# Ten two-input operations of a hybrid SSD and latent-attention layer made on GpSimd instead of VectorE

## The chip, the core and the metric

The kernel runs on one core of a Trainium2 chip. The metric is the device time in microseconds of one execution; three runs of the kernel before gave a median of 635.32 us (635.25 to 635.61). The core's engines run side by side, each through its own queue in order: TensorE (PE: matrix products, with weight loads shown apart as PEld), VectorE (DVE), ScalarE (ACT), GpSimd (POOL) and SyncE (SP, which only issues DMAs here). An instruction that needs another engine's result waits for a semaphore, and all that stands behind it on its queue waits too.

## The reference, cut to what matters

One layer of an encoder for 512 new frames and 64 frames of a running stream (576 tokens together, model width 1024): state-space heads (SSD) and latent attention side by side, then a dense SwiGLU block. The parts that the change touches:

```python
def step(h, inp):                       # one chunk of the state-space scan
    ...
    y = y + jnp.einsum('blgn,bghpn,blgh->blghp', Ck, h, jnp.exp(cum))
    last = cum[:, -1]
    w_end = jnp.exp(last[:, None] - cum) * d
    h_new = jnp.exp(last)[..., None, None] * h + jnp.einsum('blgh,blghp,blgn->bghpn', w_end, x, Bk)
    return h_new, y
...
y = y.reshape(b, T, SSD_WIDTH) * jax.nn.silu(z.astype(jnp.float32))      # the gating
y_ssd = rmsnorm(y, p['ssd_norm']).astype(x.dtype)
...
q = (rmsnorm(cq, p['q_norm']) @ p['w_uq']).reshape(b, T, MLA_HEADS, QK_NOPE + QK_ROPE)
...
x = x + jnp.concatenate([y_ssd, o], axis=-1) @ p['w_out']
```

The state `h` is multiplied by exp(last), its decay, from chunk to chunk; the scan's output is gated by silu(z), normed, and multiplied by the upper half of `w_out`. Queries and keys of each pair of heads come from products with that pair's weights.

## The kernel before, in words

All activations are kept transposed, channels on the 128 partitions and tokens along the free axis. A float32 product is made of three products of split operands: a high part (cast to the fp32r format by ScalarE) and a low part (raw minus high, by VectorE) of both weights and activations, multiplied as high x high, high x low and low x high. So every weight tile costs a ScalarE cast (line 111) and a VectorE subtraction (line 112) before it can be used, and every activation tile a ScalarE pass (line 143) and a VectorE subtraction (line 145).

The stages follow each other: the input projections and the convolution; the SSD scan; attention; the output projection; the SwiGLU block. Within a stage the order of steps comes from strings (`ORDER_SSD`, `ORDER_ATT`), in which letters stand for functions and digits for tiles. The order of instructions on each engine is then fixed by the table `ISSUE` at the end of the file: for each engine a list of numbers of its instructions in the order they were written.

The SSD scan takes five chunks of tokens, c = 4 (the 64 running frames, with a state loaded from memory) and c = 0 to 3 (128 new frames each). For a chunk:

- `chunk_a` and `chunk_e` build the decay matrix E: a select on GpSimd (line 515), exponentials on ScalarE (line 521), products on VectorE (lines 524 and 529).
- `chunk_b` multiplies on TensorE (`ps_y`, `ps_i`) and adds the results to the tile `xsd` on VectorE (lines 547, 554 and 555).
- `chunk_s` makes the next state: a product on TensorE (`ps_s`), the decay of the old state `h` by `el` (line 569) and the addition of `ps_s` (line 570), both on VectorE. For c = 0 there is no old state.
- `gate` multiplies `xsd` by the gate `sz` (line 582, VectorE), ScalarE squares the product (`ysq`, line 584), TensorE sums the squares (`ps_g`, line 587), and ScalarE copies the sums out.

Attention takes pairs of heads, p = 0 to 3. `pair_proj` loads and splits a pair's weights (`wr_pair`, `wh_pair`, `wl_pair`; q steps and k steps use them) and has GpSimd issue DMAs that put rotary rows beside the queries (line 616). `scores` multiplies queries and keys into one of three PSUM banks (`sc`), VectorE finds the maximum (`mx`, line 655), ScalarE takes the exponential and its sum (`pr`, line 656), VectorE inverts the sum (`sm`, line 657), and both engines scale (lines 662 and 660). Three banks mean that TensorE's next scores wait for ScalarE's exponential of an earlier one.

Between the first pair's scores stands the end of the state-space part: `norm_y` makes the factor `Ry`, and `cat_tile(t)`, t = 0 to 3, scales a tile of `xsd` by it (line 764, VectorE, both large inputs in SBUF) and splits it: the high part of `cat_y` on ScalarE (line 143), the low part on VectorE (line 145). The step F0 then multiplies the four tiles by the output weights (line 458, `ps_o`). Its matmuls are interleaved with others by the table.

Of the kernel before, what the change touches and what calls it, by code (L numbers as in the profile page):

```python
# [11 lines left out]
F32 = mybir.dt.float32  # L12
F32R = mybir.dt.float32r
# [6 lines left out]
P = 128  # L20
# [7 lines left out]
H = 8  # L28
# [26 lines left out]
def hybrid_layer_kernel(ctx: ExitStack, tc: tile.TileContext, a, o):  # L55
# [51 lines left out]
    def split_weights(raw, name, wp=None):  # L107

        n = raw.shape[1]
        hi, lo = (wslot(wp or wout[0], f"{z}_{name}", F32R)[:, :n] for z in ("wh", "wl"))  # L110
        act.copy(hi, raw)  # L111
        dve.tensor_tensor(lo, raw, hi.bitcast(F32), ALU.subtract)  # L112
        return hi, lo

    def weights(src, n, name):

        raw = wslot(wpool, f"wr_{name}")
        sp.dma_start(raw[:, :n], src)
        return split_weights(raw[:, :n], name)
# [21 lines left out]
    def split_scaled(s, src, g):  # L141

        act.activation(s.bitcast(F32R)[:, 0], src, AF.Copy if g is None else AF.Identity, scale=1.0 if g is None else g)
        if g is None:
            dve.tensor_tensor(s.bitcast(F32R)[:, 1], src, s[:, 0], ALU.subtract)  # L145
        else:
            dve.scalar_tensor_tensor(s.bitcast(F32R)[:, 1], src, g, s[:, 0], ALU.mult, ALU.subtract)
# [409 lines left out]
    def chunk_s(c):  # L557
# [7 lines left out]
        if h is None:  # L565
            act.copy(hn, pst)
        else:
            hv = lambda z: z.rearrange("p (h q) -> p h q", h=H)
            dve.tensor_tensor(hv(hn), hv(h), el.unsqueeze(2).to_broadcast([P, H, HD]), ALU.mult)
            dve.tensor_tensor(hn, hn, pst, ALU.add)  # L570
# [7 lines left out]
    def gate(c):  # L578
# [3 lines left out]
        dve.tensor_tensor(yv, yv, sz[:, :, tk], ALU.mult)  # L582
# [27 lines left out]
    def pair_proj(p):  # L610
        w = weights(a["w_pair"][p], 384, f"pair{p}")
# [151 lines left out]
    def cat_tile(t):  # L763
        dve.scalar_tensor_tensor(xsd[:, t], xsd[:, t], col(C_SN + t), Ry, ALU.mult, ALU.mult)
        s = slot(ypool, "a1", f"cat_y{t}")
        split_scaled(s, xsd[:, t], None)
# [558 lines left out]
98-99 93-97 70-73 86-91 104-106 100-103 110 107-109 122-126 134-135 111-115 128-133 148-153 116-121 136-141 127  # L1325
142-147 154-169 174-175 170-171 270-274 176-221 172-173 222-269 275-370 373-420 371 421-468 372 469-634 637 641-644
638-640 657-660 635-636 665-726 737-758 661-664 763 645-652 759-760 727-736 764-766 653-656 767-818 859 761-762
819-826 860-864 833-840 827-832 865-870 841-852 871-874 853-856 875-880 857-858 881-887 904-912 888 892-899 889-891
900-903 925-926 913-921 927-934 922-924 935 939-940 936-938 949-957 964-966 941 945-948 967-968 958-963 969 942-944
970-975 987 976-979 1003 980-986 991-993 988 1004-1005 1015-1021 1006-1014 1022-1024 994-996 1025-1026 1029-1034  # L1330
1043-1045 997-998 989 1000-1002 999 1046-1054 990 1035-1039 1059-1061 1040-1042 1062-1064 1027-1028 1075-1077
1081-1092 1055-1057 1078-1080 1093-1096 1058 1097-1104 1121-1123 1071-1072 1124-1129 1065 1068-1070 1073 1105-1107
1066-1067 1074 1130-1156 1119-1120 1229-1240 1157 1108-1114 1158 1241-1245 1253-1262 1246-1247 1115-1118 1159-1161
1176-1177 1248-1252 1263-1264 1162-1175 1265 1180 1178 1181-1183 1179 1266-1268 1277-1279 1184-1187 1190-1195
1269-1276 1196-1204 1188-1189 1205-1223 1227-1228 1224-1226 1280-1297 1301-1303 1298-1300 1304-1321 1342-1343
1348-1355 1344-1347 1322-1341 1356-1511 1572 1512-1559 1575-1576 1560-1571 1577 1596-1598 1578 1573-1574 1593
1584-1585 1579 1581-1583 1602-1604 1623-1625 1594-1595 1614 1586 1605-1606 1590-1592 1611-1613 1632-1634 1587-1589
1608-1610 1607 1580 1599-1601 1620-1622 1641 1626-1628 1647-1649 1642-1643 1615-1616 1635-1637 1617-1619 1638-1640
1653 1656 1658-1667 1644-1646 1629-1631 1650-1652 1654-1655 1668-1669 1657 1682 1694-1705 1683-1693 1670-1681
1730-1741 1706-1729 1742-1748 1754-1755 1749-1753 1756-1767 1778-1785 1768-1777 1786-1885 1898-1905 1886-1897  # L1340
1906-2017 2030-2036 2018-2029 2037-2053 2066-2084 2054-2065 2085-2089 2102-2104 2090-2101 2105-2221 2234-2236
2240-2241 2222-2233 2237 2242-2248 2238-2239 2249-2725 2738-2740 2744 2726-2737 2741 2745-2751 2742-2743 2752-3229
3242-3244 3248 3230-3241 3245 3249-3255 3246-3247 3256-3733 3746-3748 3752 3734-3745 3749 3753-3759 3750-3751
3760-4189
# [5 lines left out]
101-102 125 120 126-127 119 131-133 155 134 129 135-136 140-142 149 104 152 128 150 153 170 143-144 138 145 147 151  # L1350
154 156 137 146 174 157 178 159 171-172 187 169 160 158 161-162 176 206 163 175 183 180 164 167 165-166 168 215 181
177 188 173 189 182 184 190 195 191 179 192-194 197 185-186 224 196 204 207-209 198-203 214 205 210 288 211 225
216-218 212 220 222 219 213 226 221 223 227-228 233 229-230 234 231-232 235-236 245 255 246 237 294 256 247 239 248
257 259 258 260 240 238 264 241 261 242 263 262 307 267 243 265 244 266 249 268 270 251 269 253 250 274 252 254
275-276 289 271 290 277-279 295 286 280 282 281 287 272 297 317 291 283 318 273 298 302 299 316 300 284-285 319 303
306 292-293 296 309 312 304 326 305 310 308 313 327 362 311 328 322 301 323 314 363 330 324 320 329 315 336 321 325
364 333 367 337 331-332 365 340 338 334-335 341 344 349 339 350 345 342 346 352 351 343 355 358 366 347 359 357 348
360 356 353 361 368 377 354 370-371 369 372 375-376 373-374 382 390 378 384 383 385-386 379 389 387 380 397 388 381
393 405 395 391 396 394 392 400 399 401 398 403 402 420 406 404 408 407 409 412 410 417 414 411 413 418 462 416 421
423 419 464 425 422 424 415 433 431 426 432 429 428 427 438 430 434 469 463 436 435 437 439 442 441 443 466 440 444  # L1360
451 465 446 467-468 452-453 445 447 455 454 448 473 475 456 477 476 474 457 472 470 478 458-459 449-450 479 460 481
480 461 471 482 491 487 483 496-497 484 488 498-499 489 500-502 485-486 503 510 490 515-518 522 492 504 519 506 520
507 521 508 532-535 539 546 493-495 536 547-549 505 511-512 509 523 537 529-530 524-525 513-514 531 538 540 528 550
541 566 526 542 527 551 543 545 552 544 567-568 553-554 569 555 574 570 556-559 561 575-576 560 565 577 562 578-581
571 582-583 572 563 590-591 584 592 585-586 564 598 573 599-600 593-594 587-588 601 589 603 602 595 604-607 596 610
597 608-609 620-623 611 627 612 624 613-614 625-626 619 634-636 628 637 617 638 618 629 616 615 630 641 639 631 640
633 632 654-656 642 657 643 662 658 644-647 649 663-664 648 653 665 650 666-669 659 670-671 660 651 678-679 672 680
673-674 652 686 661 687-688 681-682 675-676 689 677 691 690 683 692-695 684 698 685 696-697 708-711 699 715 700 712
701-702 713-714 707 722-724 716 725 705 726 706 717 704 703 718 729 727 719 728 721 720 742-744 730 745 731 750 746
732-735 737 751-752 736 741 753 738 754-757 747 758-759 748 739 766-767 760 768 761-762 740 774 749 775-776 769-770  # L1370
763-764 777 765 779 778 771 780-783 772 786 773 784-785 796-799 787 803 788 800 789-790 801-802 795 810-812 804 813
793 814 794 805 792 791 806 817 815 807 816 809 808 830-832 818 833 819 839 834 820-823 825 840-841 824 829 842 826
843-846 835 847-848 836 827 855-856 849 857 850-851 828 864 837 865-866 858 838 859 852-853 867 854 869 868 860
870-873 861 876 862 874 880 875 881-883 887 884 863 885 877 886 879 878 888-898
""",
    "ACT": """
0-5 8 6-7 10 9 13 11 14 12 15 17-18 16 21 19 24 20 23 40 22 25 45 26-27 52 28-33 49-50 56 34-35 37 36 60 51 41-43
38-39 64 44 46-48 53-54 68 55 57-58 72 59 61-62 76 63 65-67 77 69-71 73 92 74-75 94 79 88 78 81 104 82 90 84 116 86-87
103 85 83 100 98 80 97 89 99 102 101 96 91 126 105 93 111 109-110 156 115 95 107-108 113 122 114 112 142 117 163 106
118-119 136 127 137 134 128 140 135 124 121 120 139 129 138 141 130 123 143 131 125 150 146 149 132 210 133 145 148  # L1380
154 152 151 147 158-159 157 144 155 160-162 153 164-165 212 170 172 171 166 168 180 186 169 181 174 187 175 173 176
189 167 190 177 227 178 192 179 193 188 182 195 194 191 183 200 196 184-185 199 201 197 213 208 215-216 202-203 219
# [126 lines left out]
```

## Time and profile before

| what | value |
|---|---|
| median of three runs | 635.32 us (635.25 to 635.61) |
| the profiled execution's own time | 634.82 us |
| its span, first to last instruction | 633.1 us |
| mean granted TensorE clock | 0.997 |
| GpSimd, busy | 110.9 us, 18% |
| ScalarE, busy | 400.0 us, 63% |
| VectorE, busy between 150 and 160 us | 9.94 of 10 us |

A row of a timeline gives start and duration in microseconds, engine, line, operation, output tile <- input tiles, shape and count; a bracket at its end says how long the engine stood idle before it and whose work ended that. Rows of equal instructions that follow each other are merged (x3). The wait view counts such idle times by pairs of engines. Tile names lack their numbers, so `cat_y` is any of the four tiles. VectorE's successive instructions overlap by some 0.08 us in their records. TensorE's ends are modelled.

### The profile page before, as it was taken

To read this page: it belongs to the slowest core of one execution; us is meant where nothing else is said; L and a number is where in the kernel's file an instruction comes from. 1 tells how busy PE (TensorE), PEld (TensorE's weight loads), DVE (VectorE), ACT (ScalarE), POOL (GpSimd) and SP (SyncE) were. 2 spreads that over 40 slices of the span, in tenths; PEclk is the share of its full clock that TensorE was granted. 3 is DMA by queue.
4 is the path that set the end of the run, shared out by engine and by line. 5 is a ranking of instruction groups with operands and counts; after the bars stand their busy time and mean duration, and the time that the engine had idled before them with its cause. 6 is when DMAs were issued, how large, how long until landed. Compare 5 with 4: busy or idle time off the path is not lost.

```text
span 633.1 us, 12089 instructions
## 1 busy us (share of the span) xinstructions
PE 622.9 (98%) x4635; PEld 596.2 (94%) x4635; DVE 541.9 (86%) x945; ACT 400.0 (63%) x768; POOL 110.9 (18%) x164
## 2 busy tenths in 40 slices
PE   9999999999999999999999999999999999999995
PEld 8899999886787899999999999999999999999995
DVE  6999986899776699999999888988899789976555
ACT  7655346779775567666556676566656665767364
POOL 1322103001010000001301330033104220323323
PEclk9999999999999999999999999999999999999998
DMA  8322364323231223335743986398738893689924
GB/s 320 135 61 74 96 198 122 113 75 102 81 117 34 95 73 126 88 113 172 260 131 89 217 182 156 79 191 186 172 100 161 198 204 101 101 215 256 254 38 149
DMA packets 39593, 89.19 MB, mean 141 GB/s; under 512 B 4570, under 2 KB 14312, under 8 KB 39280
## 3 DMA queue, kind: packets, MB, share of 16 engines
q1 hardware_dynamic: 26416, 63.12, 30.9%
q0 software_dynamic: 12400, 24.73, 21.4%
q8 instruction: 36, 0.59, 0.4%
q10 hardware_dynamic: 720, 0.57, 0.3%
q14 instruction: 21, 0.17, 0.1%
HBM read 62.74 MB, written 24.53 MB: 138 GB/s over the span
## 4 chain that ended last, share of the span: by engine, by line
PE 90%; DVE 5%; ACT 2%; issue 1%; POOL 1%; DMA 1%; POOLq 0%; DVEq 0%
PE ps_x L874 21%; PE ps_d L1064 14%; PE ps_z L874 10%; PE ps_in L281 8%; PE ps_o L458 5%; PE ps_y L874 5%; PE ps_z L458 4%; PE ps_first L129 3%; PE ps_d L281 2%; PE ps_p L874 2%; PE ps_l L281 2%; PE sc L672 2%; PE pv L719 1%; PE ptp L694 1%; PE ps_q L458 1%
## 5 line engine op out<-in xcount | busy, mean ns | idle before, releaser
L874 PE MATMUL ps_x<-xop,wh_gu_S 128*128 128x288 f32 x378 | 76.9, 295 | 0.0
L112 DVE TENSOR_TENSOR wl_gu_S<-gu,wh_gu_S 128x1024 fp32r<-128x1024 f32 x44 | 53.3, 1220 | 9.7 <-ACT wh_gu_S L111 6.5
L874 PEld LDWEIGHTS ps_x<-xop,wh_gu_S 128*128 128x128 f32 x378 | 60.5, 188 | 0.0
L1078 POOL DMA_DIRECT2D acc<-fz x32 | 27.9, 904 | 165.2 <-ACT fz L1075 136.5
L111 ACT CAST wh_gu_S<-gu 128x1024 fp32r<-128x1024 f32 x44 | 46.3, 1052 | 16.2 <-PE ps_y L874 8.3
L874 PE MATMUL ps_x<-xop,wl_gu_S 128*128 128x288 f32 x189 | 55.8, 295 | 0.0
L281 PE MATMUL ps_in<-xs,wh_in 128*128 128x256 f32 (+1 forms) x256 | 51.2, 296 | 0.4 <-DVE sp_a L361 0.4
L281 PEld LDWEIGHTS ps_in<-xs,wh_in 128*128 128x128 f32 x256 | 40.8, 188 | 1.2 <-issue 1.1
L281 PE MATMUL ps_in<-xs,wl_in 128*128 128x320 f32 (+1 forms) x128 | 37.7, 295 | 0.0
L874 PEld LDWEIGHTS ps_x<-xop,wl_gu_S 128*128 128x128 f32 x189 | 35.5, 188 | 0.0
L111 ACT CAST wh_gu_A<-gu 128x1024 fp32r<-128x1024 f32 x22 | 23.1, 1050 | 10.3 <-PE ps_x L874 6.9
L874 PE MATMUL ps_z<-xop,gu_a 128*128 128x288 f32 x189 | 29.5, 294 | 0.0
L458 PE MATMUL ps_o<-cat_y,wh_out 128*128 128x256 f32 (+1 forms) x128 | 29.0, 312 | 0.3 <-DVE cat_y L145 0.3
L112 DVE TENSOR_TENSOR wl_gu_A<-gu,wh_gu_A 128x1024 fp32r<-128x1024 f32 x22 | 26.8, 1218 | 1.2 <-ACT wh_gu_A L111 1.0
L874 PE MATMUL ps_x<-xop_last,wh_gu_S 128*128 128x288 f32 x126 | 26.9, 295 | 0.0
L874 PEld LDWEIGHTS ps_z<-xop,gu_a 128*128 128x128 f32 x189 | 26.5, 188 | 0.0
L1064 PE MATMUL ps_d<-pair,d_1h 128*128 128x288 f32 x128 | 26.4, 296 | 0.0
L874 PE MATMUL ps_z<-xop,wh_gu_S 128*128 128x288 f32 x126 | 26.0, 295 | 0.0
L458 PE MATMUL ps_z<-xs,wh_z 128*128 128x256 f32 (+1 forms) x128 | 25.8, 296 | 0.1
L458 PE MATMUL ps_o<-cat_o,wh_out 128*128 128x320 f32 (+1 forms) x128 | 25.5, 295 | 0.3 <-DVE x L750 0.3
L874 PE MATMUL ps_y<-xop,wh_gu_A 128*128 128x288 f32 x126 | 25.8, 296 | 0.0
L874 PE MATMUL ps_x<-xop,wh_gu_A 128*128 128x288 f32 x126 | 25.7, 295 | 0.0
(417 smaller groups left out, 2138.9 us busy)
## 6 DMA issues: line engine op xcount, KB each, us to landing
gu<-in_w_gu SPq DMA_DIRECT2D x44, 512.0 KB, 5.5
wr_d<-in_w_down SPq DMA_DIRECT2D x18, 512.0 KB, 4.0
acc<-fz POOLq DMA_DIRECT2D x16, 288.0 KB, 6.8
acc<-da POOLq DMA_DIRECT2D x16, 288.0 KB, 8.1
acc<-dc POOLq DMA_DIRECT2D x16, 288.0 KB, 8.6
wr_in<-in_w_in SPq DMA_DIRECT2D x8, 512.0 KB, 3.7
wr_out<-in_w_out SPq DMA_DIRECT2D x8, 512.0 KB, 3.3
cumb<-cumD SPq DMA_DIRECT2D x5, 512.0 KB, 4.5
```

Source lines behind the costliest of these rows:

```text
L111: act.copy(hi, raw)
L112: dve.tensor_tensor(lo, raw, hi.bitcast(F32), ALU.subtract)
L129: pe.matmul(ps[:m, hf, : cols.stop - cols.start], w, x[:, cols], start=start and k == 0 and i == 0, stop=stop and k == last and i == 2,)
L281: pe.matmul(ps, w, x[:, cols], start=first and k == 0 and i == 0, stop=last and k == len(terms) - 1 and i == 2,)
L458: pe.matmul(ps[:, :n], w, x[:, cols], start=k == 0 and i == 0, stop=k == len(terms) - 1 and i == 2,)
L672: pe.matmul(s[:, :nk], qs[:, j, q0 : q0 + P], ks[:, j, :nk], start=True, stop=True)
L694: pe.transpose(pp[:, k : k + P], prs[p, i][:, j, b * P : b * P + P], ident)
L719: pe.matmul(pv[64 * j : 64 * j + 64, b * P :], V[b][:, h * HD : (h + 1) * HD], pts[p, b, j], start=b == 0, stop=True, skip_group_check=b > 0,)
L874: pe.matmul(ps, p, q, start=not onto and first and kp == kps[0] and j == 0, stop=onto or (last and kp == kps[-1] and j == 2), skip_group_c ...
L1064: pe.matmul(ps, p, v, start=not onto and n == 0 and j == 0, stop=onto or (n == len(ks) - 1 and j == 2), skip_group_check=onto,)
L1078: pool.dma_start(out, src, accum_op=ALU.add)
```

## The change

Helpers take the engine that subtracts as an argument, and ten operations name GpSimd (`pool`):

- the gating (line 582) of chunks 4, 0 and 1; chunks 2 and 3 stay on VectorE;
- the decay of the state (line 569) for chunks 1, 2 and 3; chunk 4's stays;
- the low parts (line 112) of the weights of pairs 2 and 3;
- the low parts (line 145) of `cat_y` 0 and 2; 1 and 3 stay.

```diff
-    def split_weights(raw, name, wp=None):
+    def split_weights(raw, name, wp=None, sub=dve):
...
-        dve.tensor_tensor(lo, raw, hi.bitcast(F32), ALU.subtract)
+        sub.tensor_tensor(lo, raw, hi.bitcast(F32), ALU.subtract)
...
-    def split_scaled(s, src, g):
+    def split_scaled(s, src, g, sub=dve):
...
-            dve.tensor_tensor(s.bitcast(F32R)[:, 1], src, s[:, 0], ALU.subtract)
+            sub.tensor_tensor(s.bitcast(F32R)[:, 1], src, s[:, 0], ALU.subtract)
...
-            dve.tensor_tensor(hv(hn), hv(h), el.unsqueeze(2).to_broadcast([P, H, HD]), ALU.mult)
+            (dve if c == 4 else pool).tensor_tensor(hv(hn), hv(h), el.unsqueeze(2).to_broadcast([P, H, HD]), ALU.mult)
...
-        dve.tensor_tensor(yv, yv, sz[:, :, tk], ALU.mult)
+        (pool if c in (4, 0, 1) else dve).tensor_tensor(yv, yv, sz[:, :, tk], ALU.mult)
...
-        w = weights(a["w_pair"][p], 384, f"pair{p}")
+        w = weights(a["w_pair"][p], 384, f"pair{p}", pool if p > 1 else dve)
...
-        split_scaled(s, xsd[:, t], None)
+        split_scaled(s, xsd[:, t], None, dve if t % 2 else pool)
```

The table is rewritten to match, since instructions are numbered engine by engine. A line or two of it, GpSimd's before and after:

```diff
-0-3 7 18 28 4 8 5 9 6 10 26 11 27 12 29 13-17 20-23 19 24-25 31 30 32-42 53 55 57 59 54 56 58 60 43-52 61-69 71 73 75
+0-3 7 18 28 4 8 5 9 6 10 26 11 27 12 29 13-17 20-23 19 24-25 31 30 32-42 57 59 61 63 58 60 62 64 43-48 52-54 49-51 55-56
```

What it makes of the order: TensorE's and SyncE's instructions stand exactly as before. On GpSimd, in the SSD scan, the three gates (L582), the three decays (L569) and pair 2's low part come among the selects (`h_1651`, `h_1844` and `h_1870` are the states after chunks 1, 2 and 3):

```order
 L515 AFFINE_SELECT cumb_1598<-cumb_1598 128x1024
+L582 TENSOR_TENSOR xsd<-xsd,sz 128x4x64
+L582 TENSOR_TENSOR xsd<-xsd,sz 128x4x128
+L569 TENSOR_TENSOR h_1651<-h_1596,el_1472 128x512
 L515 AFFINE_SELECT cumb_1716<-cumb_1716 128x1024
+L582 TENSOR_TENSOR xsd<-xsd,sz 128x4x128
+L569 TENSOR_TENSOR h_1844<-h_1651,el_1600 128x512
+L569 TENSOR_TENSOR h_1870<-h_1844,el_1718 128x512
+L112 TENSOR_TENSOR wl_pair_2157<-wr_pair_2154,wh_pair_2156 128x384
 L616 DMA qs_381<-rrp 16x576 x4
```

Seven operations stand ahead of pair 2's DMA issues, which had followed the last select. Further on in GpSimd's queue, between the DMA issues of pair 2 (`qs_381`) and those of pair 3 (`qs_383`), come the tiles cat_y 0 (`cat_y_1955`) and 2 (`cat_y_1963`) and pair 3's low part:

```order
 L616 DMA qs_381<-rrp 16x576 x4
+L145 TENSOR_TENSOR cat_y_1955<-xsd,cat_y_1955 128x576
+L145 TENSOR_TENSOR cat_y_1963<-xsd,cat_y_1963 128x576
+L112 TENSOR_TENSOR wl_pair_2246<-wr_pair_2243,wh_pair_2245 128x384
 L616 DMA qs_383<-rrp 16x576 x4
```

So three operations stand ahead of pair 3's DMA issues. On VectorE, at the end of the state-space part, the scalings of the four tiles (L764) now follow each other with cat_y 1 (`cat_y_1959`) and 3 (`cat_y_2033`) behind:

```order
 L764 SCALAR_TENSOR_TENSOR xsd<-xsd,par,Ry 128x576
 L662 TENSOR_SCALAR pr_4_2013<-pr_4_2013,sm 128x320
-L764 SCALAR_TENSOR_TENSOR xsd<-xsd,par,Ry 128x576
-L145 TENSOR_TENSOR cat_y_1955<-xsd,cat_y_1955 128x576
-L764 SCALAR_TENSOR_TENSOR xsd<-xsd,par,Ry 128x576
+L764 SCALAR_TENSOR_TENSOR xsd<-xsd,par,Ry 128x576 x2
 L145 TENSOR_TENSOR cat_y_1959<-xsd,cat_y_1959 128x576
-L145 TENSOR_TENSOR cat_y_1963<-xsd,cat_y_1963 128x576
 L145 TENSOR_TENSOR cat_y_2033<-xsd,cat_y_2033 128x576
```

Two of the four subtractions are gone from there, and the third and fourth scaling are neighbours. On ScalarE one instruction moves, the cast of pair 3's weights (line 111), from ahead of the exponentials of the first pair's last new-frame scores to behind the high parts of all four `cat_y` tiles. Elsewhere the engines' orders are the same but for the ten that left VectorE.

More of the change, by code (lines that the diff above doesn't have):

```diff
@@ L111, in split_weights, with weights @@
         act.copy(hi, raw)
-        dve.tensor_tensor(lo, raw, hi.bitcast(F32), ALU.subtract)
+        sub.tensor_tensor(lo, raw, hi.bitcast(F32), ALU.subtract)
         return hi, lo
-    def weights(src, n, name):
+    def weights(src, n, name, sub=dve):
         raw = wslot(wpool, f"wr_{name}")
         sp.dma_start(raw[:, :n], src)
-        return split_weights(raw[:, :n], name)
+        return split_weights(raw[:, :n], name, sub=sub)
     UNEVEN = (slice(0, 256), slice(256, T))
@@ L1329 @@
[L1329 to L1338, printed above, removed]
@@ new lines @@
+1224-1226 1280-1297 1301-1303 1298-1300 1304-1321 1342-1343 1348-1355 1344-1347 1322-1341 1356-1511 1572 1512-1559
+1575-1576 1560-1571 1577 1596-1598 1578 1573-1574 1593 1584-1585 1579 1581-1583 1602-1604 1623-1625 1594-1595 1614 1586
+1605-1606 1590-1592 1611-1613 1632-1634 1587-1589 1608-1610 1607 1580 1599-1601 1620-1622 1641 1626-1628 1647-1649
+1642-1643 1615-1616 1635-1637 1617-1619 1638-1640 1653 1656 1658-1667 1644-1646 1629-1631 1650-1652 1654-1655 1668-1669
+1657 1682 1694-1705 1683-1693 1670-1681 1730-1741 1706-1729 1742-1748 1754-1755 1749-1753 1756-1767 1778-1785 1768-1777
@@ L1345 @@
+1786-1885 1898-1905 1886-1897 1906-2017 2030-2036 2018-2029 2037-2053 2066-2084 2054-2065 2085-2089 2102-2104 2090-2101
+2105-2221 2234-2236 2240-2241 2222-2233 2237 2242-2248 2238-2239 2249-2725 2738-2740 2744 2726-2737 2741 2745-2751
+2742-2743 2752-3229 3242-3244 3248 3230-3241 3245 3249-3255 3246-3247 3256-3733 3746-3748 3752 3734-3745 3749 3753-3759
+3750-3751 3760-4189
 """,
@@ new lines @@
+726 731 743 728 744-747 737 748-749 738 729 756-757 750 758 751-752 730 764 739 765-766 759-760 753-754 767 755 769 768
+761 770-773 762 776 763 774-775 786-789 777 793 778 790 779-780 791-792 785 800-802 794 803 783 804 784 795 782 781 796
+807 805 797 806 799 798 820-822 808 823 809 829 824 810-813 815 830-831 814 819 832 816 833-836 825 837-838 826 817
+845-846 839 847 840-841 818 854 827 855-856 848 828 849 842-843 857 844 859 858 850 860-863 851 866 852 864 870 865
+871-873 877 874 853 875 867 876 869 868 878-888
@@ new lines @@
+136 127 137 134 128 140 135 124 121 120 139 129 138 141 130 123 143 131 125 150 146 149 132 210 133 145 148 154 152 151
+147 158-159 157 144 155 160-162 153 164-165 212 170 172 171 166 168 180 186 169 181 174 187 175 173 176 189 167 190
+177-178 192 179 193 188 182 195 194 191 183 200 196 184-185 199 227 201 197 213 208 215-216 202-203 219 209 204 217 234
+218 198 205-206 211 214 226 220 233 221 240 207 223 242 224 222 241 229 243-244 225 271 235 230 228 231 238 237 272 232
+245 236 248 239 246 249-252 247 257 255 261 254 262 256 259 263 258 278 265 253 267 266 264 268-270 260 273-277 284
@@ new lines @@
+440-441 439 442-443 448 456-457 449 458 450 454 451 455 453 452 459 464 460 465-466 462 461 463 467 475 468 476 469 474
+471 473 470 483 472 484 477 492-493 479-482 485 494 487 495 488-489 486 490-491 478 496 501 498 502 497 499-500 509-510
+503 518-519 505-507 504 508 511 520 512 521 514-515 513 516-517 522 530-531 523 532 524 528 525 529 527 526 533 538 534
+539-540 536 535 537 541 549 542 550 543 548 545 547 544 557 546 558 551 566-567 553-556 559 568 561 569 562-563 560
+564-565 552 570 575 572 576 571 573-574 583-584 577 592-593 579-581 578 582 585 594 586 595 588-589 587 590-591 596
@@ L1407 @@
-72 67 65 76 69-71 78 73 86 64 74-75 87 80 88-89 84 90 85 91 98 101 99-100 102-103 106-165
+11-14 16 15 17-20 23 22 25 21 24 31 26 32 39-40 36 33 38 41-42 37 43-47 55 77 62 79 54 56 58 63 81 57 60 59 61 68 66 72
+67 65 76 69-71 78 73 86 64 74-75 87 80 88-89 84 90 85 91 98 101 99-100 102-103 106-165
 """,
```

102 lines of the change are left out of this document (42 added, 60 removed).

## The prediction

> **What bounds the kernel now.** I read the page first, for the engine that is full.
>
> ```profile
> span 633.1 us, 12089 instructions
> PE 622.9 (98%) x4635; PEld 596.2 (94%) x4635; DVE 541.9 (86%) x945; ACT 400.0 (63%) x768; POOL 110.9 (18%) x164
> ```
>
> TensorE (PE) is busy in 622.9 of 633.1 us, so VectorE's (DVE's) 86% is mostly cover. Work taken off VectorE shortens the run only where TensorE waits for it. The second view is therefore the list of TensorE's own waits, from 60 to 600 us, which leaves out the start and the tail that the change doesn't touch.
>
> ```profile
> PE sc L672 <- ACT pr L656: 1.1, 2, 0.9
> PE ps_o L458 <- DVE x L750: 0.3, 1, 0.3
> PE ps_o L458 <- DVE cat_y L145: 0.3, 1, 0.3
> PE sc_s L678 <- ACT pr L656: 0.2, 1, 0.2
> ```
>
> Each row gives total, times and longest. The first, third and fourth lie in the ten microseconds in which the state-space part hands over to attention; their sum, 1.1 + 0.3 + 0.2 = 1.6 us, or 0.25% of the run, is all that these edits can win. The second lies later, in a part that stays as it was. The third view is TensorE's timeline of the first output tile, F0, which multiplies the four gated tiles cat_y0 to cat_y3:
>
> ```profile
> 160.65 0.42 PE L458 MATMUL ps_o<-cat_y,wh_out 128*128 128x320 f32 x1 [0.31 <-DVE cat_y L145]
> ...
> 161.55 0.40 PE L458 MATMUL ps_o<-cat_y,wh_out 128*128 128x256 f32 x2
> ...
> 161.91 0.47 PE L458 MATMUL ps_o<-cat_y,wh_out 128*128 128x256 f32 x2
> ```
>
> By the program's order these use the low part of cat_y1 (160.65, after a wait of 0.31 us) and, as the second of each pair, about 0.12 us on, of cat_y2 (161.67) and of cat_y3 (162.03).
>
> **What one operation costs on GpSimd.** GpSimd (POOL) does two-input tensor operations in the tail:
>
> ```profile
> L1271 POOL TENSOR_TENSOR fz<-fz,sq 128x256 f32<-128x256 f32 x7 | 5.2, 738 | 5.5 <-ACT sq L1266 5.0
> ```
>
> ```profile
> 610.05 0.88 POOL L1222 TENSOR_TENSOR fz<-fz,sq 128x320 f32<-128x320 f32 x1 [13.73 <-ACT sq L1217]
> ```
>
> 256 columns take 0.738 us and 320 take 0.88, so one column more costs 0.142 / 64 = 2.2 ns. That makes 1.02 us for 384, 1.30 for 512 and 1.44 for 576. The other bound is growth in proportion to size, 0.738 x 576 / 256 = 1.66. I take 1.44, since two sizes show a fixed part; an estimate. GpSimd's ten operations are one of 256, five of 512, two of 384 and two of 576: 0.74 + 6.50 + 2.04 + 2.88 = 12.2 us of its time, on an engine that is busy 18%.
>
> **Whether the two engines hinder each other.** Twice a VectorE operation overlaps a select of GpSimd's, which reads SBUF (the first row is what the first select waits for):
>
> ```profile
> 108.15 0.22 ACT L490 ACTIVATE el<-cumb 128x8 f32<-128x8 f32 x1
> ```
>
> ```profile
> 108.49 1.09 POOL L515 TENSOR_SCALAR_AFFINE_SELECT cumb<-cumb 128x1024 f32<-128x1024 f32 x1 [6.30 <-ACT el L490]
> ...
> 127.41 1.09 POOL L515 TENSOR_SCALAR_AFFINE_SELECT cumb<-cumb 128x1024 f32<-128x1024 f32 x1 [11.46 <-ACT el L490]
> ```
>
> ```profile
> 108.99 1.14 DVE L112 TENSOR_TENSOR wl_uv<-wr_uv,wh_uv 128x512 fp32r<-128x512 f32 x1
> ...
> 111.17 0.67 DVE L524 TENSOR_TENSOR xw<-xdt,E 128x512 f32<-128x512 f32 x1
> ...
> 127.26 1.28 DVE L529 TENSOR_TENSOR E<-E,ps_b 128x512 f32<-128x512 f32 x2
> ```
>
> With both inputs in SBUF, 512 columns take 0.67 us undisturbed (L524), but 1.14 when GpSimd is at work (L112). 1.14 - 0.67 = 0.47, so it began in effect at 109.46, and GpSimd's operation ended at 109.58: VectorE was held until 0.12 us before GpSimd's recorded end. L529, with one input in PSUM, overlaps the second select and still takes 0.64 apiece: not held. The tail has it the other way round:
>
> ```profile
> 611.01 1.02 POOL L1222 TENSOR_TENSOR fz<-fz,sq 128x320 f32<-128x320 f32 x1
> ```
>
> ```profile
> 610.77 0.51 DVE L1227 TENSOR_TENSOR sq_last<-sq_last,sq 128x320 f32<-128x320 f32 x1 [0.23 <-ACT sq L1217]
> ```
>
> GpSimd's second took 0.14 more than its first, until 0.13 before VectorE's end (611.28). So whoever comes second waits until about 0.13 us before the other's recorded end. The Trainium skill's page "SBUF — State Buffer", section "Who interferes with whom", calls this an exclusive lock in which the second to issue "fully blocks" until the first finishes, where VectorE has two SBUF inputs. The trace agrees but for the 0.13 us. Waiting to the very end at each of the three handovers below would make the sum 0.4 us worse by that page.
>
> **The change part by part.** *Gates.* Three gates go to GpSimd; the tightest is c = 4:
>
> ```profile
> 119.80 0.75 DVE L472 SCALAR_TENSOR_TENSOR sz<-zt,zh 128x576 f32<-128x576 f32 x1
> ```
>
> ```profile
> 122.41 1.00 PE L587 MATMUL ps_g<-ysq,ones 128*128 128x64 f32 x8
> ```
>
> ```profile
> 121.04 0.42 ACT L584 ACTIVATE ysq<-xsd 128x256 f32<-128x256 f32 x1
> ```
>
> Its input is there at 120.55. GpSimd ends about 0.74 later, at 121.3, ScalarE (ACT) squares until about 121.8, and TensorE reads at 122.41: hidden with 0.6 us left. The gates of c = 0 and 1 stand further from their readers. Where they hold VectorE, its queue has slack before the next TensorE use. I count nothing; without the cover, each would cost up to 0.6 us (1.30 against the 0.68 of VectorE's 512-wide rows).
>
> *Decays.* The tightest is that of chunk 3, whose input is the state that VectorE finishes first:
>
> ```profile
> 139.22 0.68 DVE L570 TENSOR_TENSOR h<-h,ps_s 128x512 f32<-128x512 f32 x1
> 139.82 0.68 DVE L555 TENSOR_TENSOR xsd<-xsd,ecp 128x512 f32<-128x512 f32 x1
> ...
> 142.67 0.68 DVE L570 TENSOR_TENSOR h<-h,ps_s 128x512 f32<-128x512 f32 x1
> 143.26 0.68 DVE L554 TENSOR_TENSOR ecp<-ps_i,ecp 128x512 f32<-128x512 f32 x1
> ```
>
> ```profile
> 142.31 0.68 PE ps_i L553 x6
> ```
>
> L555 has the port from 139.82 to 140.37; GpSimd then runs to about 141.7. The addition of ps_s can't start before TensorE ends that product, at 142.31. So GpSimd's decay is hidden with 0.6 us left, and one of 1.9 us would still be. The decay that VectorE no longer makes stood just ahead of these rows. L570 then starts at about 142.34, and L554 waits for ps_i, at 142.99 + 0.03 = 143.02 instead of 143.26. **Gain: 0.24 us.** The rest of the decay's time turns into VectorE's wait for TensorE.
>
> *Low parts of two weights.* pair2's left VectorE at a place where it waits for ScalarE's exponentials: nothing. On GpSimd it ends near 143.8, ahead of four DMA issues that start only at 153.06:
>
> ```profile
> 153.06 2.02 POOL L616 DMA_DIRECT2D qs<-rrp  x4 [24.56 <-PE sc_s L678]
> ```
>
> pair3's removal is worth 153.85 - 153.38 = 0.47 us of VectorE, and ScalarE's cast moves behind the cat_y tiles. But the rows around it show where that stops:
>
> ```profile
> 152.86 0.28 DVE L655 TENSOR_REDUCE mx<-sc 128x1 f32<-128x128 f32 x1
> ...
> 153.38 0.55 DVE L112 TENSOR_TENSOR wl_pair<-wr_pair,wh_pair 128x384 fp32r<-128x384 f32 x1
> 153.85 0.48 DVE L655 TENSOR_REDUCE mx<-sc_s 128x1 f32<-128x320 f32 x1
> ...
> 156.03 0.16 DVE L657 RECIPROCAL sm<-sm 128x1 f32<-128x1 f32 x1
> ...
> 157.42 0.38 DVE L662 TENSOR_SCALAR pr<-pr,sm 128x320 f32<-128x320 f32 x1
> 157.72 0.81 DVE L764 SCALAR_TENSOR_TENSOR xsd<-xsd,par,Ry 128x576 f32<-128x576 f32 x1
> ...
> 159.11 0.81 DVE L764 SCALAR_TENSOR_TENSOR xsd<-xsd,par,Ry 128x576 f32<-128x576 f32 x1
> 159.84 2.09 DVE L145 TENSOR_TENSOR cat_y<-xsd,cat_y 128x576 fp32r<-128x576 f32 x3
> ```
>
> ```profile
> L145 DVE TENSOR_TENSOR cat_y<-xsd,cat_y x4: 749/750/751, 158.4 to 161.2; 128x576 fp32r<-128x576 f32 x4
> ```
>
> ```profile
> 153.17 0.37 ACT L656 ACTIVATE pr<-sc,mx 128x128 f32<-128x128 f32 x1
> ...
> 155.62 0.20 ACT L656 ACTIVATION_READ_ACCUMULATOR pr<-sc_s,mx 128x1 f32 x1
> ...
> 156.51 0.68 ACT L143 ACTIVATE cat_y<-xsd 128x576 fp32r<-128x576 f32 x1
> ```
>
> ScalarE's exponential at 153.17 starts when the maximum of 152.86 is done, ahead of pair3's low part; from there to 156.51 ScalarE works without a break. So ScalarE, and TensorE which waits for its exponentials, gain only the 0.24. VectorE gains 0.24 + 0.47 until the reciprocal, which needs ScalarE's sum: 155.82 - 0.24 + 0.03 = 155.61 instead of 156.03, a lead of 0.42. pair3's four DMA issues stand behind all this on GpSimd, but they wait for scores of pair1, which TensorE has only begun by then.
>
> *Low parts of cat_y0 and cat_y2.* Here the port decides. ScalarE ends the high part of cat_y0 at 157.19 - 0.24 = 156.95; GpSimd starts 0.12 later (as the select of 108.49 did after ScalarE's 108.37), at 157.07. Its DMA issues ended at 155.08. VectorE wants the port for the third L764 at 157.72 - 0.42 = 157.30, finds it taken until 157.07 + 1.44 - 0.13 = 158.38, and starts 0.66 us later than before. The fourth follows 0.73 later, at 159.11, and cat_y1's low part (0.75 us by the last row) at 159.84, both exactly where they were, although cat_y0's low part no longer stands between. So TensorE's product of 160.65 stays there: the 0.24 won is lost again. GpSimd's cat_y2 takes the port when VectorE's cat_y1 gives it up, 159.84 + 0.75 - 0.13 = 160.46, and ends at 161.90. With 0.06 to reach TensorE (160.59 to 160.65 above), 161.96 against 161.67: +0.29. cat_y3's low part on VectorE is held until 161.77, ends at 162.52, and TensorE has it at 162.58 against 162.03: **+0.55 us in all.** After that TensorE has no wait for a changed operation, so the shift stays.
>
> **The sum.** 0.24 won at 143 is given back by 160.65; then +0.55. The profiled execution took 634.82 us (span 633.1), 0.50 below the median of the runs, 635.32. So 635.4 on its own scale and 635.9 on the median's. A measurement of this kernel can tell about 0.2% (1.3 us) from no change, and this lies inside.
>
> **The rivals.** (1) *GpSimd's operations don't hold VectorE's.* For it: no row shows VectorE held by a GpSimd TENSOR_TENSOR for long, only by the selects. Then L764 is not held, cat_y1's low part is ready in time, and both the 0.24 and the 0.31 of TensorE's wait are won: 0.55 us less, 634.8. GpSimd's cat_y2 would end 161.04, just ahead of its use at 161.1.
>
> (2) *Slower: VectorE gets to the port first.* Its third L764 wants it 0.23 us after GpSimd; if L662 ahead of it, at 157.42 - 0.42 = 157.00 for 0.38, keeps GpSimd off as well, that lead shrinks to 0.07. The same section of the Trainium skill's "SBUF — State Buffer" lists tensor_scalar, which L662 is, among those that can take the pair; no run here shows it. If VectorE wins, L764 ends at 158.11, GpSimd has cat_y0 from 157.98 to 159.42, the fourth L764 is held to 159.29 and ends 160.10; GpSimd then slips cat_y2 in, from 159.97 to 161.41, ahead of cat_y1's low part, which ends at 162.03. TensorE gets it at 162.09 instead of 160.65: +1.44 us, 636.8. It decides from 0.23 us of delay at GpSimd's start.
>
> (3) *GpSimd's time grows in proportion to size.* At 1.66 us for 576 columns the same steps give cat_y1 at +0.2, cat_y2 ending 162.3, cat_y3 162.9: +0.97, 636.3.
>
> (4) *All of TensorE's waits go.* 1.6 us less, 633.7; against it, ScalarE's unbroken run after 153.17.
>
> **How the numbers follow.** Forecast 0.44; rival 1, 0.17; rival 2, 0.18; rival 3, 0.17; rival 4, 0.04. The range reaches from just under rival 1 to just over rival 2, 634.7 to 636.9. Faster by over 0.2% is rival 4 alone, 0.04; slower is rival 2, 0.18; the rest, 0.78, lies within.
>
> **What would show it.** In the changed profile, L145 on GpSimd with 1.44 us; the third L764 with a duration of 1.9 instead of 0.81; TensorE waiting about 0.3 for cat_y2 from GpSimd and 0.2 for cat_y3. Rival 1 shows L764 at 0.81 throughout, rival 2 GpSimd's cat_y0 starting after the third L764. A wait of TensorE on a gate, a decay or a pair weight would prove my "hidden" wrong.

## The result, and the profile after

The changed kernel took 644.47 us (median of 4 runs, 643.93 to 645.23) against 635.47 for the kernel before (4 runs, 635.25 to 636.25): a ratio of 1.0145, 95% interval 1.0133 to 1.0158, or 9.0 us slower. The prediction, 635.9 us and no change that can be told, was wrong, and its range (to 636.9) with it. The profiled execution took 643.93 us, its span 642.0, 8.9 more than before.

The page's busy times, and the granted clock in 40 slices of the span (tenths of full speed):

```profile
PE 625.2 (97%) x4635; PEld 597.8 (93%) x4635; DVE 538.8 (84%) x935; ACT 400.4 (62%) x768; POOL 124.3 (19%) x174
...
PEclk9999999999799999999999999999999999999999
```

VectorE is busy 3 us less and GpSimd 13 more; the ten operations had taken VectorE 6.4 us by their rows, so part of what it was spared came back as time in which it is held (below). TensorE, with the same work, is busy 2.3 us more, and one slice, 160.5 to 176.6 us, has a lower clock. That is where to look. TensorE's own waits come next, by the view and the window (60 to 600 us) that the prediction read; the columns are total, times and longest.

```profile
PE ps_q L458 <- DVE x L750: 6.1, 1, 6.1
PE sc L672 <- ACT pr L656: 1.1, 2, 0.9
PE ps_o L458 <- DVE cat_y L145: 0.7, 1, 0.7
```

The wait for a `cat_y` tile (the last row: `cat_y1`, 0.3 us before) grew by 0.4 us, where the prediction had it unchanged. The first row is new: a single wait of 6.1 us, and it names L750, which adds the output projection to the tile `x` and which the change does not touch. Set beside each other, TensorE's same instructions show where the time went. Before:

```profile
163.25 0.31 PE L458 MATMUL ps_o<-cat_y,wl_out 128*128 128x320 f32 x1
163.39 0.43 PE L458 MATMUL ps_q<-cqn,wh_pair 128*128 128x288 f32 x2
...
165.03 0.60 PE L672 MATMUL sc<-ks,qs 100*128 100x256 f32 x2
...
623.94 0.61 PE L1236 MATMUL ps_n<-ones,fz 128*128 128x1 f32 x4 [0.66 <-POOL fz L1271]
```

After:

```profile
164.14 0.31 PE L458 MATMUL ps_o<-cat_y,wl_out 128*128 128x320 f32 x1
170.54 0.85 PE L458 MATMUL ps_q<-cqn,wh_pair 128*128 128x288 f32 x2 [6.09 <-DVE x L750]
...
173.56 0.60 PE L672 MATMUL sc<-ks,qs 100*128 100x256 f32 x2
...
632.83 0.61 PE L1236 MATMUL ps_n<-ones,fz 128*128 128x1 f32 x4 [0.66 <-POOL fz L1271]
```

The delay is 0.89 us at the end of the `cat_y` tiles, 7.15 at the next matmul, 8.53 some 1.6 us of work later, and 8.89 near the end. TensorE was 0.19 late already at 119 us, ahead of the first changed operation (119.01 before, 119.20 after), and level with the kernel before at 147.7 us (147.71 and 147.72). So 0.19 was won in the scan, the tiles cost 0.89, the wait costs 6.26, another 1.38 is lost while TensorE is at work again, and 0.36 comes piecemeal later.

Who made VectorE late? Its row of the timeline names a DMA:

```profile
170.06 0.42 DVE L750 TENSOR_TENSOR x<-ps_o,x 128x256 f32<-128x256 f32 x1 [6.63 <-DMA x<-in_xT]
```

SyncE's queue shows that DMA and what stands ahead of it, before:

```profile
153.96 0.33 SPq L118 DMA_DIRECT2D wr_out<-in_w_out  x1
154.34 0.42 SPq L772 DMA_DIRECT2D x<-in_xT  x1
```

and after:

```profile
163.72 0.33 SPq L118 DMA_DIRECT2D wr_out<-in_w_out  x1
164.10 0.42 SPq L772 DMA_DIRECT2D x<-in_xT  x1
```

The load of `x` goes out 9.76 us later, because the load of the next output weights in front of it does. SyncE's waits after, from 143 to 165 us, say for whom:

```profile
SPq L118 <- POOL wl_pair L112: 17.5, 2, 17.3
```

The load of `wr_out` writes into the buffer in which the raw weights of pair 3 lie, so it waits for their last reader. Before, that was VectorE's subtraction (153.38 for 0.55 in the prediction's rows): it ended at 153.93, and the load left 0.03 later. Now it is GpSimd's, behind two `cat_y` tiles, and its ScalarE cast stands behind four. GpSimd's and ScalarE's rows after:

```profile
157.28 1.63 POOL L145 TENSOR_TENSOR cat_y<-xsd,cat_y 128x576 fp32r<-128x576 f32 x1 [2.18 <-ACT cat_y L143]
160.32 1.89 POOL L145 TENSOR_TENSOR cat_y<-xsd,cat_y 128x576 fp32r<-128x576 f32 x1 [1.41 <-ACT cat_y L143]
162.17 1.52 POOL L112 TENSOR_TENSOR wl_pair<-wr_pair,wh_pair 128x384 fp32r<-128x384 f32 x1
```

```profile
160.87 0.50 ACT L111 CAST wh_pair<-wr_pair 128x384 fp32r<-128x384 f32 x1
```

162.17 + 1.52 = 163.69, and 0.03 later the load leaves. Nobody needs pair 3's low part yet; what is needed is its input buffer. VectorE's rows at the port, after:

```profile
157.25 0.38 DVE L662 TENSOR_SCALAR pr<-pr,sm 128x320 f32<-128x320 f32 x1
157.55 2.70 DVE L764 SCALAR_TENSOR_TENSOR xsd<-xsd,par,Ry 128x576 f32<-128x576 f32 x2
160.17 2.65 DVE L145 TENSOR_TENSOR cat_y<-xsd,cat_y 128x576 fp32r<-128x576 f32 x2
```

Two L764 take 2.70 and two L145 2.65 instead of about 1.5 for each two: VectorE and GpSimd keep each other from SBUF, as the prediction's port step had it. TensorE's first product for which that matters, at 160.65 after 0.31 us of waiting before, now reads as in the first row here; the other two are the pairs whose second matmul uses `cat_y2` and `cat_y3`, and which took 0.40 and 0.47 before:

```profile
160.97 0.42 PE L458 MATMUL ps_o<-cat_y,wh_out 128*128 128x320 f32 x1 [0.66 <-DVE cat_y L145]
...
161.86 0.79 PE L458 MATMUL ps_o<-cat_y,wh_out 128*128 128x256 f32 x2
...
162.61 0.66 PE L458 MATMUL ps_o<-cat_y,wh_out 128*128 128x256 f32 x2
```

The 1.38 us after the wait is TensorE's clock. The columns after each stretch and its length are the busy time of PE, PEld, DVE, ACT and POOL, the granted clock, and the DMA share and GB/s:

```profile
163.27:166.68 3.41, 1.18 (x9) 0.90 (x8) 0.15 (x1) 0.00 (x0) 0.42 (x1) 1.00 0.54 180
166.68:170.09 3.41, 0.00 (x0) 0.00 (x0) 0.03 (x1) 0.00 (x0) 0.00 (x0) 0.50 0.77 320
170.09:173.50 3.41, 2.96 (x11) 2.82 (x12) 3.30 (x8) 1.62 (x5) 0.00 (x0) 0.50 0.00 0
173.50:176.91 3.41, 3.41 (x23) 2.68 (x22) 1.54 (x5) 3.08 (x9) 0.00 (x0) 1.00 0.00 0
```

The granted clock halves 2.2 us after TensorE ran dry and stays so for 6.82 us, of which TensorE is at work for the last 2.96.

### The profile page after: what moved, and what is told of

Same layout as the page of the kernel before. It is cut to its first block, busy times and chain, and to the rows that moved or that the text cites. A ratio compares the mean times of both kernels' runs of the same rounds, so it can differ in the third digit from the quotient of the medians.

```text
span 642.0 us, 12099 instructions
## 1 busy us (share of the span) xinstructions
PE 625.2 (97%) x4635; PEld 597.8 (93%) x4635; DVE 538.8 (84%) x935; ACT 400.4 (62%) x768; POOL 124.3 (19%) x174
## 4 chain that ended last, share of the span: by engine, by line
PE 87%; DVE 5%; ACT 3%; POOL 2%; issue 2%; DMA 1%; POOLq 0%; ACTq 0%; DVEq 0%
PE ps_x L874 21%; PE ps_d L1064 14%; PE ps_z L874 10%; PE ps_in L281 7%; PE ps_y L874 5%; PE ps_o L458 4%; PE ps_z L458 4%; PE ps_first L129 3%; PE ps_d L281 2%; PE ps_p L874 2%; PE ps_l L281 2%; PE sc L672 2%; PE pv L719 1%; PE ptp L694 1%; PE ps_q L458 1%
## 5 line engine op out<-in xcount | busy, mean ns | idle before, releaser
L1023 POOL DMA_DIRECT2D acc<-dn x8 | 4.4, 545 | 121.5 <-ACT dn L1022 121.5
```

Source lines behind the costliest of these rows:

```text
L1023: pool.dma_start(acc[1][t], dn)
```

## The experiments

Theory A: the raw buffer and SyncE's queue make the load of `x` late, and the clock follows. Theory B: GpSimd's operations hinder the others by the port or otherwise, and the load is late with them. Each ratio is to the kernel before, in the same series, with its 95% interval.

### Four kernels with a second difference

In the first four kernels GpSimd's `drain` (line 1161), which the kernel before and the changed kernel have behind GpSimd's last accumulating DMAs (line 1159), stood at the start of GpSimd's queue. It computes nothing, and the expectations below don't know of it.

`x2_first`, SyncE's order:

```diff
 DMA wr_pair (pair 3)
+DMA x (L772)
 DMA wr_out (L118)
-DMA x (L772)
 DMA wr_out (L118)
```

> The changed kernel, with one instruction moved: on SyncE the load of x's third tile (L772) stands ahead of the load of the output weights (L118 wr_out) instead of behind it. Nothing else differs. Theory A (the raw weight tiles share one buffer, so the wr_out load waits for GpSimd's pair3 low part, and x's load waits behind it on SyncE's queue): x is loaded some 20 us earlier, TensorE's 6.1 us wait for L750 and the drop of its clock behind it go, the 0.55 to 0.7 of the cat_y tiles stay: about 636.1 us (635.7 to 636.9). Theory B (GpSimd's operations hinder VectorE, or load the chip so that TensorE's clock drops, and the transfer is only late with them): GpSimd's work is the same, so the time stays at 643 to 645.

`pair3_back`, with the ScalarE cast at its old place:

```diff
-        w = weights(a["w_pair"][p], 384, f"pair{p}", pool if p > 1 else dve)
+        w = weights(a["w_pair"][p], 384, f"pair{p}", pool if p == 2 else dve)
```

> The changed kernel with one of its ten operations undone: the low part of pair3's weights (L112) is made on VectorE again, and its cast on ScalarE stands where it stood before. The other nine stay on GpSimd. Theory A (shared raw buffer and SyncE's queue): the wr_out load goes out near 154 again, x with it, and only the cat_y cost is left: about 636.1 us (635.7 to 636.9). Theory B (the time is lost to the two cat_y subtractions on GpSimd and to the port): 643 to 645. TensorE's wait for L750 tells them apart too: 0 by A, about 6 us by B.

`pair3_alone`, against the kernel before (`pair3_early` is the same with the ScalarE cast at its old place):

```diff
-        w = weights(a["w_pair"][p], 384, f"pair{p}")
+        w = weights(a["w_pair"][p], 384, f"pair{p}", pool if p == 3 else dve)
```

> The kernel before with one of the ten operations: only the low part of pair3's weights goes to GpSimd, with its ScalarE cast behind the cat_y tiles as in the changed kernel. Theory A: the low part ends near 162.2 us (no cat_y subtraction ahead of it), the load of x goes out near 162.7 and lands near 168.5, TensorE waits about 5 us for L750, and its clock drops behind that: 640.5 to 642.5 us, most of the loss by this one 1 us operation. Theory B (port or GpSimd's load): one operation more on GpSimd costs at most its own 1 us: 635 to 636.5.

> As the run before (only pair3's low part on GpSimd), but with the ScalarE cast at its old place, ahead of the exponentials. Theory A: GpSimd makes the low part right behind its DMA issues, near 155.1 to 156.2, so the load of x goes out near 156.6 and lands near 162.4, about when TensorE needs its bank: 635.2 to 636.3 us. So the loss is a matter of when the operation ends, not of the engine that does it. Theory C (the operation on GpSimd is costly wherever it stands, by its longer time or the port): about the same as with the late cast, 640 or more.

Measured, with 635.31 us for the kernel before: `x2_first` 640.10 (1.0076, 1.0061 to 1.0091), `pair3_back` 639.93 (1.0068, 1.0053 to 1.0083), `pair3_alone` 646.67 (1.0185, 1.0168 to 1.0202), `pair3_early` 639.64 (1.0064, 1.0049 to 1.0079). TensorE's 6.1 us wait was gone in the first, second and fourth and there in the third, as A has it, but all four lay some 4 to 5 us above what the expectations had. The end of the trace shows why. The rows are GpSimd's last drains (shortest, median and longest in ns), of `x2_first`:

```profile
L1507 POOLq DRAIN  x3: 46/98/7049, 630.4 to 638.0; - x3
```

and of the kernel before:

```profile
L1496 POOLq DRAIN  x3: 34/93/1513, 628.2 to 632.8; - x3
```

The drain at the kernel's end takes 7.05 us instead of 1.51, and the other engines wait for it. With `drain` back in its place the four kernels were run again; each came out 3.5 to 3.9 us shorter.

### The load of x moved ahead

> The run x2_first with GpSimd's drain (L1161) back behind its last additions, where the kernel before and the changed kernel have it; in x2_first and its three sisters it had slipped to the start of GpSimd's queue, and GpSimd's last drain took 7.05 us instead of 1.51. So here the only edit to the changed kernel is the load of x's third tile ahead of the wr_out load on SyncE. Theory A (shared raw buffer, SyncE's queue): 1.0 to 1.4 us over the kernel before, 636.3 to 636.9. Theory B (GpSimd's operations hinder the rest, the clock drops because of them): 643 to 645. Theory D (the 3 us that x2_first lost at its end are the changed kernel's own, not the drain's): 639.5 to 640.5 again, with a last drain of 7 us.

Measured: 636.39 us, 1.0024 (1.0014 to 1.0033). Theory A. SyncE's rows:

```profile
144.11 0.41 SPq L772 DMA_DIRECT2D x<-in_xT  x1
163.41 8.93 SPq L118 DMA_DIRECT2D wr_out<-in_w_out  x2
```

The second row merges two loads. The first of them, that of `wr_out` at 163.41, is as late as in the changed kernel (163.72) and hurts nobody. From 160 to 175 us TensorE has one wait left:

```profile
PE ps_o L458 <- DVE cat_y L145: 0.7, 1, 0.7
```

Ten operations on GpSimd and the order of one load: 7.8 of the 9.0 us are gone, the half clock at 166 us too. Theory B, as the cause of the 9 us, and theory D (the 3 us at the end are the changed kernel's own) fall.

### One operation of the ten

> The run pair3_alone with GpSimd's drain where the kernel before has it: one operation of ten moves to GpSimd, the low part of pair3's weights, with the late ScalarE cast. Theory A: the load of x goes out near 163.2 us as in pair3_alone, TensorE idles some 6 us for L750, its clock drops behind it: 643 to 644, nearly all of the changed kernel's loss by one operation of 1 us. Theory B: 635 to 636.5.

Measured: 643.20 us, 1.0130 (1.0117 to 1.0144), 8.1 us of the 9.0. GpSimd's and SyncE's rows:

```profile
160.81 1.68 POOL L112 TENSOR_TENSOR wl_pair<-wr_pair,wh_pair 128x384 fp32r<-128x384 f32 x1 [5.88 <-ACT wh_pair L111]
```

```profile
162.51 0.33 SPq L118 DMA_DIRECT2D wr_out<-in_w_out  x1
162.89 0.42 SPq L772 DMA_DIRECT2D x<-in_xT  x1
```

Again the load leaves 0.02 after the operation's end, and TensorE waits 6.1 us for L750. Here GpSimd is not late through its own work: it waits for ScalarE's cast. So this run changes two things, the engine and the place of the cast; the next leaves the cast where it was.

> The run pair3_early with GpSimd's drain where the kernel before has it: only pair3's low part on GpSimd, with the ScalarE cast where it was. Theory A: the load of x goes out near 156.3 us and lands just in time: 635.3 to 636.5. Theory C (this operation on GpSimd is costly wherever it stands): 640 or more.

Measured: 635.99 us, 1.0016 (1.0007 to 1.0025). The same operation on the same engine, ended 6.5 us sooner, costs 0.85 us instead of 8.1, so theory C falls. A late cast alone is enough for the loss; in the changed kernel the two `cat_y` tiles stand ahead of the operation as well, and whether they alone would be enough was not run. The rest, 0.85, is put down to the port. VectorE's and GpSimd's rows:

```profile
154.70 1.34 DVE L662 TENSOR_SCALAR pr<-pr,sm 128x128 f32<-128x128 f32 x1
```

```profile
154.93 1.01 POOL L112 TENSOR_TENSOR wl_pair<-wr_pair,wh_pair 128x384 fp32r<-128x384 f32 x1
```

L662 takes 1.34 us instead of 0.28. By the records it began 0.23 us ahead of GpSimd's operation and was held all the same, while GpSimd's took no longer than pair 2's low part does with nothing in its way (1.01). So the prediction's "whoever comes second waits" doesn't fit the recorded starts here, and why is open. ScalarE's first `cat_y` pass, which needs what follows L662, makes TensorE wait 0.5.

### Nine of the ten

> The run pair3_back with GpSimd's drain where the changed kernel has it: the changed kernel with pair3's low part back on VectorE, its ScalarE cast at the old place, nine operations on GpSimd. Theory A: the raw buffer comes free near 153.7 us, nothing waits for the load of x, the cost of the cat_y tiles is left: 635.8 to 636.4. Theory B (the nine others carry a part of the loss): 638 or more.

Measured: 636.04 us against 635.25, 1.0012 (1.0003 to 1.0021): theory A; the nine others together cost 0.8 us.

### The two cat_y tiles alone

Edit to the kernel before: `split_scaled(s, xsd[:, t], None, dve if t % 2 else pool)`, and nothing else.

> The kernel before with two of the ten operations: only the low parts of cat_y 0 and 2 on GpSimd. It prices the step of the prediction that was worked out for +0.55 us (VectorE and GpSimd keep each other from SBUF; here without the 0.24 + 0.47 of lead that the other eight give). By the lock: VectorE reaches its third L764 near 157.7 us and GpSimd's cat_y0 starts near 157.3, so it is held until near 158.6; the four tiles end some 0.9 to 1.4 us later for TensorE: 636.0 to 636.9. Without a lock: cat_y1 is ready sooner, TensorE's wait of 0.31 goes: 635.0 to 635.4.

Measured: 636.12 us, 1.0017 (1.0008 to 1.0026), 1.0 us more: by the lock. The number was right, the place was not. VectorE's rows:

```profile
157.33 1.53 DVE L662 TENSOR_SCALAR pr<-pr,sm 128x320 f32<-128x320 f32 x1
158.78 1.53 DVE L764 SCALAR_TENSOR_TENSOR xsd<-xsd,par,Ry 128x576 f32<-128x576 f32 x2
```

GpSimd's tile began at 157.18, ahead of L662, and it is L662 that is held, for 1.53 - 0.38 = 1.15 us; the two L764 behind it run free. TensorE, which transposes what L662 scales, waits 0.9 for it. The prediction noted that no run showed a tensor_scalar at the lock; this one does, as does `pair3_early_again`. It agrees with the list in the Trainium skill's "SBUF — State Buffer", section "Who interferes with whom".

### The seven operations of the scan, and two attempts to beat both kernels

`scan_and_pair2`: gates, decays and pair 2's low part on GpSimd, the rest as before.

> The kernel before with seven of the ten operations on GpSimd: three gates, three decays, pair2's low part. By the prediction's steps they are hidden and worth 0.24 us or less: 634.7 to 635.2, no change that can be told. If an operation of GpSimd's longer time reaches TensorE somewhere, TensorE's waits name it and the time is above 635.5.

Measured: 635.05 us against 635.25, 0.9993 (0.9984 to 1.0002). Hidden, as forecast. In the trace TensorE wins 0.19 us between 119 and 147 us and loses 0.69 between 163.2 and 165 us (this execution, 635.69 us, was the slowest of its 11), with this row of VectorE's:

```profile
162.99 0.42 DVE L750 TENSOR_TENSOR x<-ps_o,x 128x256 f32<-128x256 f32 x1 [0.81 <-DMA x<-in_xT]
```

The load had left at 153.98, and landed 8.9 us later. So the load of `x` had no slack in the kernel before either: its two loads of `x` landed 8.2 and 8.4 us after their issue, the first then no sooner than 154.34 + 8.2 = 162.54, and L750 began at 162.65. How long the load takes differs between runs, from 5.5 to 8.9 us for this one.

> Meant to beat both kernels: the same seven operations on GpSimd; pair3's low part on VectorE, but behind the low parts of the cat_y tiles, where nothing waits for it, with its late ScalarE cast; and x's third tile loaded ahead of wr_out on SyncE, so that nothing that TensorE needs stands behind pair3's raw buffer. All four cat_y low parts on VectorE. VectorE then has a lead of some 0.4 us at the cat_y tiles without GpSimd in the way: TensorE's wait of 0.31 and some of the rest goes: 634.4 to 634.9. If TensorE's time there is set by ScalarE, which works without a break from 153 to 157 us, nothing is won: 635.0 to 635.3.

Measured: 635.40 us, 1.0001 (0.9992 to 1.0010). Not won, and above both ranges of the expectation. VectorE's 0.55 us for pair 3, put behind the tiles, now stand ahead of a copy and of L750 (161.65 for 0.55, then L696 at 162.12 instead of 161.85), and 0.30 of the 0.38 us won between 73 and 161 us go there.

> The run scan_and_pair2 (seven operations on GpSimd, pair3's low part on VectorE at its old place) with x's third tile loaded ahead of wr_out on SyncE. In scan_and_pair2 VectorE waited 0.81 us and TensorE 0.3 us for this load, which landed near 162.9: the kernel before has next to no slack there either. If that wait is what the 0.2 to 0.35 us won by the decays was lost to, TensorE now has no wait for L750 near 163 us and the time is 634.6 to 634.9 us, 0.3 to 0.6 below the kernel before; if not, 635.0 to 635.3 as scan_and_pair2. The difference is at the limit of what the measurement tells; the wait in the trace decides.

Measured: 634.91 us against 635.19, 0.9995 (0.9986 to 1.0004). TensorE's wait for L750 near 163 us is gone; of the 0.2 us won in the scan nothing is lost there. No kernel here is faster than the one before by what can be told.

## Why the prediction was wrong

**The step that failed** stands at pair 3's low part. The prediction asked who waits for its result, and for GpSimd's DMA issues behind it ("they wait for scores of pair1"), and let the step end there. It did not ask who waits for its input. Moving a subtraction moves the release of the raw tile that it reads; the next load into that buffer stands on SyncE, and behind it in the same queue the load of `x`, which VectorE, a PSUM bank and TensorE wait for in turn. So "After that TensorE has no wait for a changed operation, so the shift stays" led to a wrong sum: the 6.1 us wait is for an unchanged operation, some links away. The prediction named ScalarE's later cast in the same step and gave it no price; it is part of what made the release late (10 us, from 153.93 to 163.69). `x2_first_again` shows the link by the queue (7.8 us won back by one load's place), `pair3_alone_again` and `pair3_early_again` the link by the buffer (8.1 and 0.85 us for one operation at two places). What the profile of before had to offer was SyncE's row at 153.96, 0.03 us behind the end of the subtraction: a load that leaves as an operation ends is waiting for it.

**The wait for L750 that the prediction set aside** is not this one. It said of `ps_o <- DVE x L750: 0.3` that it "lies later, in a part that stays as it was", and so it does, before and after:

```profile
248.79 0.56 PE L458 MATMUL ps_o<-cat_o,wh_out 128*128 128x320 f32 x2 [0.33 <-DVE x L750]
```

```profile
257.21 0.56 PE L458 MATMUL ps_o<-cat_o,wh_out 128*128 128x320 f32 x2 [0.30 <-DVE x L750]
```

The 6.1 us wait, at `ps_q`, had no row in the list of before, so going through the waits that are there could not find it. What was there was a load with no slack (`scan_and_pair2` above).

**The clock** had no term. The half clock cost 1.38 us behind the wait. It follows from the wait: with the wait gone the clock at 166 us stays at 1.00.

**The port step was right in mechanism and near in size.** It forecast +0.55 at the last tile; after allowing for the 0.19 already there at 119 us, TensorE was 0.70 late. From `cat_y1` to `cat_y2` and on to `cat_y3` the delay grew by 0.27 and 0.26, forecast 0.29 and 0.26; what was missed is 0.13 at `cat_y1`, forecast in place. GpSimd's 576 columns took 1.43 us where nothing held them (`pair3_back_again`), forecast 1.44; the third L764 was held 1.16 us, forecast 1.08. That difference is rival 2's first half: L662 (157.25 for 0.38) did keep GpSimd's first tile off, which took 1.63. Its second half, VectorE ahead of GpSimd at the third L764, did not come. (By the prediction's own 0.13 the lead left there is 157.30 - 157.25 = 0.05, not 0.07; nothing hangs on it.)

**The decays** forecast 0.24, and were given back. VectorE's rows after:

```profile
140.01 0.68 DVE L555 TENSOR_TENSOR xsd<-xsd,ecp 128x512 f32<-128x512 f32 x1
...
143.26 0.69 DVE L554 TENSOR_TENSOR ecp<-ps_i,ecp 128x512 f32<-128x512 f32 x1
```

That is 3.25 us from one to the other, against 143.26 - 139.82 = 3.44 before: 0.19. Given back, yes. **Gates and pair 2's low part**: hidden, as forecast (`scan_and_pair2`).

The price of the ten: pair 3's low part alone, with its late cast, 8.1 us, the two tiles alone 1.0, the seven others alone -0.2; the sum, before rounding, is 8.8, measured 9.0. The three have intervals of 0.6 to 0.9 us each way, so that the sum fits this closely is partly luck.

**Left open**: the 0.36 us that the changed kernel loses after 174 us, bit by bit, were not followed, and why the load of `x` takes 5.9 us to land in the changed kernel and 8.9 in `scan_and_pair2` was not tried.

## What to carry to other kernels

For each operation that moves, follow its inputs as well as its output: which load or write takes the buffer next, what stands behind that on its in-order queue, and how much slack that has. A DMA issue that begins some hundredths of a microsecond after an operation's end is a sign of such a link. Here two repairs took most of the loss away: moving the urgent load ahead of the waiting one (636.39 us) and moving the operation and its cast back (636.04).

## What the runs showed of the hardware

In the runs looked at, the granted clock changed at steps of 3.41 us, and a stretch in which TensorE has work for part of the time can be followed by one at half of it. In the changed kernel the stretch ahead of the half clock had 1.18 us of matmuls. In `pair3_back_again` it had more:

```profile
151.30:154.71 3.41, 2.26 (x10) 0.99 (x10) 3.35 (x12) 3.37 (x13) 1.57 (x4) 1.00 0.06 13
154.71:158.13 3.42, 3.42 (x8) 1.61 (x7) 3.42 (x9) 2.54 (x7) 1.23 (x2) 0.50 0.99 318
```

There TensorE was busy for 2.26 of 3.41 us by its modelled ends; 0.05 us behind the kernel before as the next stretch began, it was 0.98 behind at the end of it (158.45 against 157.47). But the kernel before has a stretch that is as full, and keeps its clock:

```profile
151.75:155.16 3.41, 2.27 (x9) 0.87 (x8) 3.38 (x13) 3.37 (x12) 1.96 (x4) 1.00 0.24 40
155.16:158.58 3.42, 3.19 (x19) 2.02 (x17) 3.42 (x9) 3.35 (x10) 0.00 (x0) 1.00 0.93 339
```

So the busy time of a stretch does not decide it by these records, and what does is open. The Trainium skill's "TensorE: Matmul & The Clock Gate", section "Part 1: The HAM clock gate", gives a free-running window of 3413 ns, with which the steps agree, and half speed after at least one idle window, with which they don't: a partly idle one did. Where the steps fall against the waits differs from run to run, so some tenths of a microsecond come and go by themselves.

GpSimd's time goes by more than the number of columns: 512 columns took 1.28 us in a gate but 1.04 in a decay, whose second input is 8 values per partition, each used 64 times. And with a `drain` behind the accumulating DMAs, which lasts 15.6 us in the kernel before while others work, GpSimd's drain at the kernel's end took 1.51 us; without it, 7.05.
